# The opening of a hybrid attention and RG-LRU block in an order written by hand: x first, modulation on ScalarE, bias as a weight column, fewer activation tables

## The chip, the core and the metric

One core of a Trainium2 chip runs the whole program. The metric is the device time of one execution in microseconds (us); less is better. TensorE is called PE, VectorE DVE, ScalarE ACT, GpSimd POOL, SyncE SP, as the profile does. Of each kernel several executions are timed, and one execution is profiled, which leaves a trace.

## What is computed

The block takes x (1024 tokens by 1024 channels), a condition vector c and a set of weights. The part that the change touches is the beginning: the RMS norm, the modulation by c, and the first columns of the big projection.

```python
mod = c @ w_ada + b_ada
shift, scale, gate = jnp.split(mod, 3, axis=-1)
h = rmsnorm(x, norm_g) * (1.0 + scale[:, None, :]) + shift[:, None, :]
proj = h @ w_in                       # 1024 x 6656
q, k, v, g_attn, xr, g_rnn, m_attn, m_rnn = jnp.split(proj, SPLIT_POINTS, axis=-1)
q = partial_rope(q, positions)        # angles of positions: sin and cos of 8 frequencies
k = partial_rope(k, positions)
...                                   # window attention with sinks, conv and RG-LRU, gates
x = x + gate[:, None, :] * (merged @ w_out)
return rmsnorm(x, final_g)
```

All values are f32.

## The kernel before, in words

**Products.** A product in full precision is made of three products of the type fp32r. Each operand is split into a high part (a cast) and a low part (the operand less its high part): `wh` and `wl` of the weights (`cast`, L101 and L103 on ACT; `rest`, L107 and L109 on DVE), `hh` and `hl` of the activations. A chunk of 128 output columns over 128 input channels is wh·hh, wl·hh and wh·hl, each for two halves of 512 tokens: six matmuls (`mm_k`, L168). In names of tiles an a or a b behind hh or hl is the half of tokens, and a number at the end counts tiles.

**The opening, L178 to L355.** SP loads four small arrays (positions, frequencies, a table of parameters `pk`, the row c), then the eight tiles of x (128 tokens by 1024 channels each), weights of the modulation `w_ss` and weights of the projection. Every x tile is squared and summed (L309 on ACT for even tiles, L311 on DVE for odd ones), the mean is taken (L314), its root on ACT (L316), the reciprocal and the scaling on DVE (L317, L318). PE transposes the tiles 128 by 128 (L323), ACT copies the results to `xT[kc]` (L325): channels kc·128 to kc·128+127 on the partitions, tokens along the row. DVE computes the rope angles in 29 small instructions (L239 to L299), ACT their sine (L328), and DMAs on POOL's queue write the table out (L331 on).

Then, for each of the eight channel chunks kc, `modulate` (L217) makes shift and scale: two DVE instructions, each multiplying a tile of `w_ss` by c and summing along the row (L220), and two single-column ones that add the bias and the norm gain (L225, L228). DVE applies them to `xT[kc]` (L344), ACT casts the two halves to hh (L347), DVE subtracts for hl (L349), and PE adds this chunk's share to three chunks of output columns, the *starts*: `w_main` 0 and 1 (the keys) and 2 (the first of the queries, scaled by 0.125). For kc up to 5 that is twelve matmuls with hh and six with hl at a time; kc 6 and 7 come last, one start after the other. A chunk kc takes 18 matmuls.

The order in which each engine of the opening runs its instructions is decided by a scheduler, which works from a model of durations and may also pull later instructions forward. From L360 on (`manual_schedule`) every engine runs in the order in which the code is written.

**What follows.** POOL makes differences of `xT` (`differences`, L381 to L384). The weights of v are split; `now` (L578 on) applies the rope to the starts (ACT L424, L425; DVE L426, L430, L431); `v_product` multiplies for v (L1259 to L1261: 96 matmuls in two calls); then the bulk of the projection is done with products of half-size blocks (`product`, L505), in fixed slots, and attention, RG-LRU and the output follow.

A few lines of the opening's end in before:

```python
for hf in range(2):
    last = A.copy(hh[kc][hf], xT[kc][:, SL[hf]])
for hf in range(2):
    V.tensor_tensor(out=hl[kc][hf], in0=xT[kc][:, SL[hf]], in1=f32(hh[kc][hf]), op=ALU.subtract)
if kc < 6:
    for w, ps in starts:
        mm_k(ps, w, kc, terms="h")
    for w, ps in starts:
        mm_k(ps, w, kc, terms="l")
```

Of the kernel before, what the change touches and what calls it, by code (L numbers as in the profile page):

```python
# [12 lines left out]
F32 = mybir.dt.float32  # L13
# [3 lines left out]
BF16 = mybir.dt.bfloat16  # L17
# [5 lines left out]
P = 128  # L23
S = 1024
# [27 lines left out]
def tile_hybrid_block(ctx, tc, x, pk, rows, posr, posi, invf, c_row, w_ss, w_gate, w_main, w_v,  # L52
# [4 lines left out]
    def dma(dst, src, eng=nc.sync):  # L57
        dst, src = (a.bitcast(F32) if a.dtype == F32R else a for a in (dst, src))
        return eng.dma_start(dst, src)  # L59
# [26 lines left out]
    def pcol(base, i):  # L86
        return pk_t[:, base + i:base + i + 1]
# [85 lines left out]
    def new_ps():  # L173
        t = psm.tile([P, 1024], F32, tag="main", name="pmain")
        return [t[:, SL[0]], t[:, SL[1]]]


    with ExitStack() as st:  # L178
        sp = st.enter_context(tc.tile_pool(name="start", bufs=1, side="right"))
        posr_t = sp.tile([P, 64], I32, name="posr_t")  # L180
        dma(posr_t[:], posr)
        invf_t = sp.tile([P, 1], F32, name="invf_t")
        dma(invf_t[:], invf)
        dma(pk_t[:], pk)
        make_identity(nc, ident)

        c_row_t = sp.tile([1, D], F32, tag="xt", name="c_row_t", bufs=10)
        dma(c_row_t[:], c_row)
        one_row = sp.tile([1, P], F32, name="one_row")
        V.memset(one_row[:], 1.0)  # L190
        c_bc = sp.tile([P, D], F32, name="c_bc")
        for hf in range(2):
            T.matmul(bk[hf], one_row[:], c_row_t[:, SL[hf]], start=True, stop=True)
            A.copy(c_bc[:, SL[hf]], bk[hf])

        xt = []
        starts = []
        wada = {}

        def load_ss(kc):  # L200
            for a in range(2):
                wa_t = sp.tile([P, D], F32, tag="xt", name="wada", bufs=10)
                dma(wa_t[:], w_ss[a * D + kc * P:a * D + (kc + 1) * P, :])
                wada[kc, a] = wa_t

        def load_xt(i):
            t = sp.tile([P, D], F32, tag="xt", name="xt", bufs=10)
            dma(t[:], x[i * P:(i + 1) * P, :])
            xt.append(t)

        mods = sp.tile([P, 16], F32, name="mods")
        gsc = sp.tile([P, 8], F32, name="gsc")
        bsc1 = sp.tile([P, 8], F32, name="bsc1")
        V.tensor_scalar(out=bsc1[:], in0=pk_t[:, PK_BSC:PK_BSC + 8], scalar1=1.0, scalar2=None,
                        op0=ALU.add)

        def modulate(kc):  # L217
            for a in range(2):
                jk = sp.tile([P, D], BF16, tag="junk2", name="jk")
                V.scalar_tensor_tensor(out=jk[:], in0=wada[kc, a][:], scalar=1.0, in1=c_bc[:],  # L220
                                       op0=ALU.mult, op1=ALU.mult,
                                       accum_out=mods[:, a * 8 + kc:a * 8 + kc + 1])
            shf = mods[:, kc:kc + 1]
            g1 = gsc[:, kc:kc + 1]
            V.scalar_tensor_tensor(out=g1, in0=mods[:, 8 + kc:9 + kc],  # L225
                                   scalar=bsc1[:, kc:kc + 1], in1=pcol(PK_NG, kc),
                                   op0=ALU.add, op1=ALU.mult)
            V.tensor_tensor(out=shf, in0=shf, in1=pcol(PK_BSH, kc), op=ALU.add)  # L228
            return g1, shf

        def load_start(i):
            w = load_w(w_main[i], 0.125 if i == 2 else 1.0)
            starts.append((w, new_ps() if i < 2 else bk[2:]))

        def tiny(name, n=64):
            return sp.tile([P, n], F32, name=name)
# [14 lines left out]
        def sub(name, a, b, n=64):  # L251
            t = tiny(name, n)
            V.tensor_tensor(out=t[:], in0=a, in1=b, op=ALU.subtract)
            return t
# [10 lines left out]
        def weighted(name, which):  # L265
            t = tiny(name)
            for i, (piece, unit) in enumerate(pieces):
# [4 lines left out]
                else:  # L272
# [1 line left out]
                                           op0=ALU.mult, op1=ALU.add)  # L274
            return t

        sa = weighted("sa", 0)
        ra = rnd("ra", sa[:], 1.0)
        fa = sub("fa", sa[:], ra[:])
        sb = weighted("sb", 1)  # L280
        tt = tiny("tt")
        V.tensor_tensor(out=tt[:], in0=fa[:], in1=sb[:], op=ALU.add)
        rt = rnd("rt", tt[:], 1.0)
        ft = sub("ft", tt[:], rt[:])
        sc_ = weighted("sc_", 2)
        V.scalar_tensor_tensor(out=sc_[:], in0=a00[:], scalar=1.0 / (2.0 * math.pi),
                               in1=sc_[:], op0=ALU.mult, op1=ALU.add)
        trn = sp.tile([P, 2, 64], F32, name="trn")
        V.tensor_tensor(out=trn[:, 1, :], in0=ft[:], in1=sc_[:], op=ALU.add)
        V.tensor_scalar(out=trn[:, 0, :], in0=trn[:, 1, :], scalar1=0.25, scalar2=None,  # L290
                        op0=ALU.add)
        trf = trn[:].rearrange("p a t -> p (a t)")
        r2 = rnd("r2", trf, 1.0, 128)
        V.tensor_tensor(out=trf, in0=trf, in1=r2[:], op=ALU.subtract)
        V.tensor_scalar(out=trf, in0=trf, scalar1=2.0 * math.pi, scalar2=3.1415925,
                        op0=ALU.mult, op1=ALU.min)
        V.tensor_scalar(out=trf, in0=trf, scalar1=-3.1415925, scalar2=None, op0=ALU.max)
        for i in range(8):
            load_xt(i)  # L299
        load_ss(0)  # L300
        load_start(0)
        ss = tiny("ss", 8)
        rr = tiny("rr", 8)
        for hf in range(2):
            for i in range(hf * 4, hf * 4 + 4):
                junk = sp.tile([P, D], BF16, tag="junk", name="junk")
                r1 = rr[:, i:i + 1]
                if i % 2 == 0:
                    A.activation(junk[:], xt[i][:], AF.Square, accum_out=ss[:, i:i + 1])  # L309
                else:  # L310
                    V.scalar_tensor_tensor(out=junk[:], in0=xt[i][:], scalar=1.0,  # L311
                                           in1=xt[i][:], op0=ALU.mult, op1=ALU.mult,
                                           accum_out=ss[:, i:i + 1])
                V.tensor_scalar(out=r1, in0=ss[:, i:i + 1], scalar1=1.0 / D, scalar2=EPS,  # L314
                                op0=ALU.mult, op1=ALU.add)
                A.activation(r1, r1, AF.Sqrt)  # L316
                V.reciprocal(r1, r1)  # L317
                xsc = V.tensor_scalar(out=xt[i][:], in0=xt[i][:], scalar1=r1, scalar2=None,  # L318
                                      op0=ALU.mult)
            for kc in range(KC):  # L320
                pt = bk[kc % (2 if hf else 4)]
                for j in range(4):
                    T.transpose(pt[:, j * P:(j + 1) * P],  # L323
                                xt[hf * 4 + j][:, kc * P:(kc + 1) * P], ident[:])
                A.copy(xT[kc][:, SL[hf]], pt)  # L325
        csn = sp.tile([P, 3, 64], F32, name="csn")
        with tc.issue_after(xsc.ins):
            A.activation(csn[:, 0:2, :].rearrange("p a t -> p (a t)"), trf, AF.Sin)  # L328
        V.tensor_scalar(out=csn[:, 2, :], in0=csn[:, 1, :], scalar1=-1.0, scalar2=None,
                        op0=ALU.mult)  # L330
        for a in range(3):  # L331
            dma(cs_d[a * 8:(a + 1) * 8, :].rearrange("f (b t) -> (f b) t", b=16),
                csn[:, a, :], G)
        dma(cs4_d, cs_d.unsqueeze(1).to_broadcast([24, 4, S]), G)

        for kc in range(KC):
            if kc == 0:
                load_start(1)
                load_start(2)
            else:  # L340
                load_ss(kc)
            with tc.issue_after(xsc.ins):
                g1, shf = modulate(kc)
            V.tensor_scalar(out=xT[kc][:], in0=xT[kc][:], scalar1=g1, scalar2=shf,  # L344
                            op0=ALU.mult, op1=ALU.add)
            for hf in range(2):
                last = A.copy(hh[kc][hf], xT[kc][:, SL[hf]])  # L347
            for hf in range(2):
                V.tensor_tensor(out=hl[kc][hf], in0=xT[kc][:, SL[hf]], in1=f32(hh[kc][hf]),  # L349
                                op=ALU.subtract)  # L350
            if kc < 6:
# [4 lines left out]
        done = None  # L356
        for w, ps in starts:
            with tc.issue_after(done.ins) if done else nullcontext():
                for kc in (6, 7):
                    done = mm_k(ps, w, kc)  # L360


    order = ExitStack()
    ET = mybir.EngineType
    order.enter_context(tc.manual_schedule(engines={ET.PE, ET.Activation, ET.DVE, ET.Pool,
                                                    ET.SP}))


    hn = pool(h_ctx, "hn")
# [905 lines left out]
    for i in range(4):  # L1275
        differences(i)
    place(pairs)
    rv = [load_half(w_v[i // 2][:, SL[i % 2]]) for i in range(4)]
# [309 lines left out]
def arrange(inputs):  # L1588
# [46 lines left out]
```

## Time and profile before

| what | value |
|---|---|
| median of 3 executions | 944.1 us (943.53 to 944.49) |
| the profiled execution | 944.47 us |
| its span, first to last instruction | 942.5 us, so 1.97 us lie outside |
| granted TensorE clock | 0.999 |
| PE busy over the span | 908.1 us, 96% |

The page of the profile gives the busy time of each engine, then its busy tenths in 40 slices of 23.6 us, then the groups of instructions by line. A row of a group has the line, the engine, the operation, out<-in by the program's names, partitions x elements, a count, the busy us, the mean ns of one, and after the second bar the idle time of the engine just before them with what ended it. A row of the timeline has the start in us, the duration in us, engine, line, operation, the names, and in brackets the idle time before it and its releaser. A row of the windows has the stretch, its length, then busy us and (count) for PE, PEld, DVE, ACT and POOL, the granted clock, the busy share of the DMA engines and GB/s.

### The profile page before, as it was taken

To read this page: it belongs to the slowest core of one execution; us is meant where nothing else is said; L and a number is where in the kernel's file an instruction comes from. 1 tells how busy PE (TensorE), PEld (TensorE's weight loads), DVE (VectorE), ACT (ScalarE), POOL (GpSimd) and SP (SyncE) were. 2 spreads that over 40 slices of the span, in tenths; PEclk is the share of its full clock that TensorE was granted. 3 is DMA by queue.
4 is the path that set the end of the run, shared out by engine and by line. 5 is a ranking of instruction groups with operands and counts; after the bars stand their busy time and mean duration, and the time that the engine had idled before them with its cause. 6 is when DMAs were issued, how large, how long until landed. Compare 5 with 4: busy or idle time off the path is not lost.

```text
span 942.5 us, 12419 instructions
## 1 busy us (share of the span) xinstructions
PE 908.1 (96%) x4261; PEld 750.6 (80%) x4261; DVE 688.8 (73%) x1068; ACT 528.8 (56%) x1036; POOL 89.7 (10%) x129
## 2 busy tenths in 40 slices
PE   5899999999999999999999999989999999999997
PEld 3689777788888788888888778867888888887886
DVE  7977798876668955984688677888999737656522
ACT  7434654455556755866585775877888632212311
POOL 1056000000000000000000000233333300000000
PEclk9999999999999999999999999999999999999999
DMA  8923565753332433352334237897666286436321
GB/s 312 370 68 152 184 223 202 268 189 125 112 112 96 139 136 100 133 212 80 122 112 168 100 134 261 278 342 251 215 198 187 67 304 219 168 118 235 128 79 67
DMA packets 84275, 164.19 MB, mean 174 GB/s; under 512 B 12771, under 2 KB 33251, under 8 KB 84214
## 3 DMA queue, kind: packets, MB, share of 16 engines
q1 hardware_dynamic: 83350, 161.09, 49.8%
q0 software_dynamic: 720, 2.07, 0.6%
q8 instruction: 33, 0.54, 0.2%
q14 instruction: 28, 0.23, 0.1%
q10 hardware_dynamic: 144, 0.26, 0.1%
HBM read 114.00 MB, written 49.78 MB: 174 GB/s over the span
## 4 chain that ended last, share of the span: by engine, by line
PE 75%; ACT 4%; DMA 4%; DVE 4%; issue 2%; SPq 0%; POOL 0%; DVEq 0%; ACTq 0%
PE bk L505 39%; PE rp L168 12%; PE rp L1500 5%; PE pgate L778 5%; PE pmain L1500 4%; PE pmain L168 4%; PE s_ps L1016 3%; PE pv L1088 3%; PE pt L1054 1%; DMA dv<-dv_d 1%; DMA ks<-k_d 1%; DMA r<-w_rp 1%; ACT wh L101 1%; DMA r<-w_main 1%; DVE nl L390 1%
## 5 line engine op out<-in xcount | busy, mean ns | idle before, releaser
L505 PE MATMUL bk<-nh,wl 128*128 128x512 f32 x368 | 143.7, 391 | 2.0 <-DVE wl L107 1.9
L505 PE MATMUL bk<-nh,wh 128*128 128x512 f32 x368 | 143.4, 390 | 0.0
L505 PE MATMUL bk<-nl,wh 128*128 128x512 f32 x368 | 143.2, 389 | 0.0
L107 DVE TENSOR_TENSOR wl<-r,wh 128x512 fp32r<-128x512 f32 x108 | 79.1, 736 | 16.5 <-ACT wh L101 16.5
L101 ACT CAST wh<-r 128x512 fp32r<-128x512 f32 x108 | 66.5, 618 | 33.5 <-DMA r<-w_ap 11.3
L505 PEld LDWEIGHTS bk<-nh,wl 128*128 128x128 f32 x368 | 69.1, 188 | 17.7 <-DVE wl L107 3.1
L505 PEld LDWEIGHTS bk<-nh,wh 128*128 128x128 f32 x368 | 69.1, 188 | 15.2 <-ACT wh L103 0.9
L505 PEld LDWEIGHTS bk<-nl,wh 128*128 128x128 f32 x368 | 69.1, 188 | 14.3
L505 PE MATMUL bk<-hh,wl 128*128 128x512 f32 x184 | 71.7, 390 | 0.4 <-DVE wl L107 0.4
L505 PE MATMUL bk<-hl,wh 128*128 128x512 f32 x184 | 71.6, 389 | 0.0
L505 PE MATMUL bk<-hh,wh 128*128 128x512 f32 x184 | 71.6, 389 | 0.0
L107 DVE TENSOR_TENSOR wl<-ws,wh 128x512 fp32r<-128x512 f32 x80 | 54.1, 683 | 4.0 <-ACT wh L101 4.0
L101 ACT CAST wh<-ws 128x512 fp32r<-128x512 f32 x80 | 48.2, 616 | 4.8 <-DVE ws L527 3.0
L1040 ACT ACTIVATE p<-p,small 128x129 f32<-128x129 f32 x128 | 50.1, 400 | 0.0
L59 POOL DMA_DIRECT2D yh_d<-yh x1 | 0.6, 583 | 482.3 <-ACT yh L835 482.3
L505 PE MATMUL bk<-hha,wl 128*128 128x512 f32 x92 | 36.4, 395 | 5.9 <-DVE wl L107 4.4
L505 PEld LDWEIGHTS bk<-hh,wl 128*128 128x128 f32 x184 | 34.5, 188 | 7.9 <-DVE wl L107 0.8
L505 PEld LDWEIGHTS bk<-hh,wh 128*128 128x128 f32 x184 | 34.5, 188 | 7.2
L505 PEld LDWEIGHTS bk<-hl,wh 128*128 128x128 f32 x184 | 34.5, 188 | 7.1
L1016 PE MATMUL s_ps<-ks,qs 128*128 128x256 f32 (+1 forms) x256 | 37.5, 289 | 0.0
L1517 ACT ACTIVATE o<-xo 128x1024 f32<-128x1024 f32 (+2 forms) x10 | 8.9, 889 | 48.4 <-DVE xo L1516 48.4
L505 PE MATMUL bk<-hla,wh 128*128 128x512 f32 x92 | 35.9, 390 | 0.0
(338 smaller groups left out, 2231.7 us busy)
## 6 DMA issues: line engine op xcount, KB each, us to landing
r<-w_main SPq DMA_DIRECT2D x100, 256.0 KB, 4.0
wada<-w_ss SPq DMA_DIRECT2D x16, 512.0 KB, 8.6
qs<-q_d SPq DMA_DIRECT2D x16, 512.0 KB, 5.4
ks<-k_d SPq DMA_DIRECT2D x24, 192.0 KB, 4.1
xt<-x SPq DMA_DIRECT2D x8, 512.0 KB, 7.2
q_d<-rhi SPq DMA_DIRECT2D x16, 256.0 KB, 3.5
q_d<-rlo SPq DMA_DIRECT2D x16, 256.0 KB, 3.3
wg<-w_gate SPq DMA_DIRECT2D x8, 512.0 KB, 5.0
```

What stands on the lines that cost most here:

```text
L101: A.copy(dst[0][:], src)
L107: V.tensor_tensor(out=dst[1][:], in0=src, in1=f32(dst[0][:]), op=ALU.subtract)
L168: mm = T.matmul(ps[hf], ww, xx[kc][hf], start=(kc == 0 and ww is w_h and xx is xh), stop=(kc == KC - 1 and xx is xl))
L390: V.tensor_tensor(out=nl[t][:], in0=xT[t][:], in1=f32(nh[t][:]), op=ALU.subtract)
L505: W["pe"] = T.matmul(ps, ww[:, c], b[kc][xx_], start=(first and kc == 0 and i == 0), stop=(kc == 3 and i == 2), skip_group_check=not first)
L778: W["pe"] = T.matmul(ps[:, SL[hf]], ww[:, c0:c0 + P], xx_[:, SL[hf]], start=(ic == 0 and i == 0), stop=(ic == 1 and i == 2))
L1016: W["pe"] = T.matmul(o, qs[:, j, qc], ks[:, b, k0 + (0 if n else P):k0 + 256], start=(b == 0), stop=(b == 1))
L1040: A.activation(px[:, j, :], px[:, j, :], AF.Exp, bias=sm[:, 0, j:j + 1], accum_out=sm[:, 1, j:j + 1])
L1054: W["pe"] = T.transpose(pt[:, j, :], px[:, j, 0:P], ident[:])
L1088: W["pe"] = T.matmul(pv[:], b, m[:].rearrange("p j q -> p (j q)"), start=(i == 0), stop=(i == len(prods) - 1))
L1500: T.matmul(ps[:, sl], lhs[k][th][:, ts_], w[:, sl], start=(k == 0 and w is h_ and lhs is mh), stop=(k == KC - 1 and lhs is ml))
L1517: A.activation(o[:, sl], xo[:, sl], AF.Square, accum_out=fs[:, i:i + 1])
```

## The change

The whole opening is put under `manual_schedule`, so that every engine runs it in the order written. In that order:

- The four small loads go to ACT's DMA queue; on SP the eight x tiles are first, then `w_ss` for kc 0, the first halves of the starts' weights, `w_ss` for kc 1 and 2; the rest is issued in the loop.
- The row of `w_ss` has 1025 numbers, the last one the bias, and c has a 1 behind it, so the row sum contains the bias: the addition L228 and the preparation L214 go. The tiles xt and wada are 1025 wide (rows of 4100 bytes).
- The squares of tiles 1 and 7 move from DVE to ACT, which does six of eight. A root of one number (L224 of the changed kernel) stands ahead of them.
- Shift and scale are applied on ACT: `cast_h` makes hh for both halves directly from the raw `xT` with Identity, scale and bias, and then a third, 1024 wide Identity writes `xT` itself, from which DVE's `low_h` subtracts. DVE's L344 goes.
- Of the 29 small rope instructions 21 move into `turns()`, at the end of kc = 3 on DVE; the sine and the table's DMAs move into `table()` at kc = 4.
- The second token half's transposes of chunks 2 to 7 move into the loop, four after each chunk's matmuls; `modulate` runs two chunks ahead; the second halves of the starts' weights are split in kc = 1, 2, 3.
- Being under the same manual order, the matmuls of v stay behind the starts.

```diff
+    order.enter_context(tc.manual_schedule(engines={ET.PE, ET.Activation, ET.DVE, ET.Pool,
+                                                    ET.SP}))
...
+        dma(c_row_t[:], c_row, A)
+        dma(posr_t[:], posr, A)
+        dma(invf_t[:], invf, A)
+        dma(pk_t[:], pk, A)
...
+                wa_t = sp.tile([P, D + 1], F32, tag="xt", name="wada", bufs=10)
...
+        for i in range(8):
+            load_xt(i)
+        load_ss(0)
+        load_wh(0, 0)
+        load_wh(1, 0)
+        load_ss(1)
+        load_wh(2, 0)
+        load_ss(2)
...
+        A.activation(root[:], one_row[:, 0:1], AF.Sqrt)
+        c_bc = sp.tile([P, D + 1], F32, name="c_bc")
+        V.memset(c_bc[:, D:], 1.0)
...
-            V.tensor_tensor(out=shf, in0=shf, in1=pcol(PK_BSH, kc), op=ALU.add)
...
-            V.tensor_scalar(out=xT[kc][:], in0=xT[kc][:], scalar1=g1, scalar2=shf,
-                            op0=ALU.mult, op1=ALU.add)
...
+        def cast_h(kc):
+            for hf in range(2):
+                A.activation(hh[kc][hf], xT[kc][:, SL[hf]], AF.Identity,
+                             scale=gsc[:, kc:kc + 1], bias=mods[:, kc:kc + 1])
+            A.activation(xT[kc][:], xT[kc][:], AF.Identity, scale=gsc[:, kc:kc + 1],
+                         bias=mods[:, kc:kc + 1])
...
+        for a in range(2):
+            modulate(0, a)
+        high(0, 0)
+        cast_h(0)
+        for i in range(3):
+            if i:
+                high(i, 0)
+            low(i, 0)
...
+        for a in range(2):
+            modulate(1, a)
+        for kc in range(KC):
+            low_h(kc)
+            if kc == 0:
+                load_ss(3)
+                for i in range(3):
+                    load_wh(i, 1)
+            if kc < 4:
+                load_ss(kc + 4)
+            elif kc == 4:
+                rv = [load_half(w_v[i // 2][:, SL[i % 2]]) for i in range(3)]
+            if kc in (1, 2, 3):
+                high(kc - 1, 1)
+            if kc + 1 < KC:
+                cast_h(kc + 1)
+            if kc + 2 < KC:
+                for a in range(2):
+                    modulate(kc + 2, a)
+            if kc in (1, 2, 3):
+                low(kc - 1, 1)
+                starts[kc - 1][0].append(W0[kc - 1, 1])
+            if kc == 3:
+                turns()
+            if kc == 4:
+                table()
             if kc < 6:
                 for w, ps in starts:
                     mm_k(ps, w, kc, terms="h")
                 for w, ps in starts:
                     mm_k(ps, w, kc, terms="l")
+            if kc + 2 < KC:
+                turn(1, kc + 2)
+                evict(1, kc + 2)
...
-    a["w_ss"] = np.ascontiguousarray(w_ada[:, :2048].T)
+    a["w_ss"] = np.concatenate([w_ada[:, :2048].T, b_ada[:2048, None]], axis=1)
```

The order of DVE where the loop begins (jk is the unused product of a modulation sum, mods and gsc are shift and scale), in before:

```order
L220 SCALAR_TENSOR_TENSOR jk,mods<-wada,c_bc 128x1024
L107 TENSOR_TENSOR wl<-r,wh 128x512
L220 SCALAR_TENSOR_TENSOR jk,mods<-wada,c_bc 128x1024
L228 TENSOR_TENSOR mods<-mods,pk_t 128x1
L107 TENSOR_TENSOR wl<-r,wh 128x512 x2
L225 SCALAR_TENSOR_TENSOR gsc<-mods,bsc_219,pk_t 128x1
L107 TENSOR_TENSOR wl<-r,wh 128x512
L109 SCALAR_TENSOR_TENSOR wl<-r,wh 128x512
L344 TENSOR_SCALAR xT<-xT,gsc,mods 128x1024
L220 SCALAR_TENSOR_TENSOR jk,mods<-wada,c_bc 128x1024
L349 TENSOR_TENSOR hla_160<-xT,hha_158 128x512
```

The same place on DVE in the changed kernel:

```order
L235 SCALAR_TENSOR_TENSOR jk,mods<-wada,c_bc 128x1025 x2
L239 SCALAR_TENSOR_TENSOR gsc<-mods,pk_t 128x1
L107 TENSOR_TENSOR wl<-r,wh 128x512 x2
L109 SCALAR_TENSOR_TENSOR wl<-r,wh 128x512
L235 SCALAR_TENSOR_TENSOR jk,mods<-wada,c_bc 128x1025 x2
L239 SCALAR_TENSOR_TENSOR gsc<-mods,pk_t 128x1
L367 TENSOR_TENSOR hla_160<-xT,hha_158 128x512
```

Five low halves of weights and the affine L344 stood ahead of the first hl; now three low halves and the whole modulation of the next chunk do.

The same engine later, at the end of kc = 3 in the changed kernel, where hl_175 is the low part of chunk 4 (the 21 small instructions, of which the first three and the last two are shown in two pieces):

```order
L235 SCALAR_TENSOR_TENSOR jk,mods<-wada,c_bc 128x1025 x2
L239 SCALAR_TENSOR_TENSOR gsc<-mods,pk_t 128x1
L109 SCALAR_TENSOR_TENSOR wl<-r,wh 128x512
L278 TENSOR_SCALAR sa<-t_260 128x64
L281 SCALAR_TENSOR_TENSOR sa<-t_264,sa 128x64
L281 SCALAR_TENSOR_TENSOR sa<-t_268,sa 128x64
```

```order
L305 TENSOR_TENSOR trn<-trn,r_575 128x128
L306 TENSOR_SCALAR trn<-trn 128x128
L308 TENSOR_SCALAR trn<-trn 128x128
L367 TENSOR_TENSOR hl_175<-xT,hh_174 128x512 x2
L235 SCALAR_TENSOR_TENSOR jk,mods<-wada,c_bc 128x1025 x2
```

Before, nothing but a modulation, the affine and now and then a low half of a weight stood between the hl of two chunks.

On ACT, at the beginning of the loop in the changed kernel:

```order
L101 CAST wh<-r 128x512
L360 ACTIVATE hha_158<-xT,mods,gsc 128x512
L360 ACTIVATE hhb_159<-xT,mods,gsc 128x512
L362 ACTIVATE xT<-xT,mods,gsc 128x1024
L101 CAST wh<-r 128x512
L103 ACTIVATE wh<-r 128x512
L360 ACTIVATE hha_162<-xT,mods,gsc 128x512
```

The high parts of the second and third start's weights stand behind the three modulating instructions of chunk 0.

More of the change, by code (lines that the diff above doesn't have):

```diff
@@ L180, in tile_hybrid_block @@
         posr_t = sp.tile([P, 64], I32, name="posr_t")
-        dma(posr_t[:], posr)
         invf_t = sp.tile([P, 1], F32, name="invf_t")
[L183 to L194, printed above, removed]
+        c_row_t = sp.tile([1, D], F32, name="c_row_t")
+        dma(c_row_t[:], c_row, A)
+        dma(posr_t[:], posr, A)
+        dma(invf_t[:], invf, A)
+        dma(pk_t[:], pk, A)
         xt = []
         starts = []
-        wada = {}
+        wada, halfw = {}, {}
         def load_ss(kc):
             for a in range(2):
-                wa_t = sp.tile([P, D], F32, tag="xt", name="wada", bufs=10)
+                wa_t = sp.tile([P, D + 1], F32, tag="xt", name="wada", bufs=10)
                 dma(wa_t[:], w_ss[a * D + kc * P:a * D + (kc + 1) * P, :])
@@ L211, in tile_hybrid_block @@
         mods = sp.tile([P, 16], F32, name="mods")
         gsc = sp.tile([P, 8], F32, name="gsc")
[L213 to L229, printed above, removed]
@@ L326, in tile_hybrid_block @@
[L326 to L334, printed above, removed]
@@ L355, in tile_hybrid_block @@
                     mm_k(ps, w, kc, terms="l")
-        done = None
+            if kc + 2 < KC:
+                turn(1, kc + 2)
+                evict(1, kc + 2)
         for w, ps in starts:
[L358 to L366, printed above, removed]
+            for kc in (6, 7):
+                mm_k(ps, w, kc)
     hn = pool(h_ctx, "hn")
```

179 lines of the change are left out of this document (120 added, 59 removed).

## The prediction

> **What bounds the kernel now.** I read the page first: the engines' totals and PE's tenths over the span.
>
> ```profile
> PE 908.1 (96%) x4261; PEld 750.6 (80%) x4261; DVE 688.8 (73%) x1068; ACT 528.8 (56%) x1036; POOL 89.7 (10%) x129
> PE   5899999999999999999999999989999999999997
> ```
>
> PE is busy nearly everywhere but in the first slices, which are the opening. So the end moves by the change in PE's idle time, and the opening is where that can change. The windows split it at the first matmul of a start, the last one, the first L505 product and a point behind it.
>
> ```profile
> 0.00:28.21 28.21, 16.38 (x69) 11.44 (x69) 23.49 (x77) 22.00 (x44) 3.35 (x10) 1.00 0.88 326
> 28.21:67.97 39.76, 37.30 (x170) 29.74 (x169) 35.33 (x70) 12.23 (x22) 9.40 (x12) 1.00 0.57 213
> 67.97:99.32 31.35, 31.35 (x219) 29.38 (x218) 25.30 (x27) 17.68 (x28) 18.60 (x13) 1.00 0.35 127
> 99.32:119.82 20.50, 17.30 (x74) 13.36 (x72) 14.76 (x23) 12.15 (x21) 0.00 (x0) 1.00 0.63 217
> 119.82:942.50 822.68, 805.78 (x3735) 666.70 (x3735) 589.92 (x875) 464.74 (x924) 58.39 (x95) 1.00 0.50 168
> ```
>
> After 119.82 PE is busy for 805.78 of 822.68 us, in an order that the change leaves alone, so I let a shift at 119.82 stand to the end. In the loop (28.21 to 67.97) PE idles only 2.46 us, with DVE almost as full (35.33 of 39.76).
>
> The groups of DVE and ACT up to 68 us price what is moved.
>
> ```profile
> L220 DVE SCALAR_TENSOR_TENSOR jk<-wada,c_bc 128x1024 bf16<-128x1024 f32 x16 | 19.5, 1218 | 0.0
> L344 DVE TENSOR_SCALAR xT<-xT,gsc,mods 128x1024 f32<-128x1024 f32 x8 | 6.5, 806 | 0.0
> L349 DVE TENSOR_TENSOR hl<-xT,hh 128x512 fp32r<-128x512 f32 x8 | 5.3, 685 | 0.7 <-ACT hh L347 0.7
> L109 DVE SCALAR_TENSOR_TENSOR wl<-r,wh 128x512 fp32r<-128x512 f32 x2 | 1.4, 685 | 0.0
> L228 DVE TENSOR_TENSOR mods<-mods,pk_t 128x1 f32<-128x1 f32 x8 | 1.2, 153 | 0.0
> ```
>
> ```profile
> L101 ACT CAST wh<-r 128x512 fp32r<-128x512 f32 x8 | 4.8, 624 | 3.7 <-PE pmain L168 3.7
> L309 ACT ACTIVATE junk<-xt 128x1024 bf16<-128x1024 f32 x4 | 4.2, 1048 | 4.4 <-DMA xt<-x 4.4
> L316 ACT ACT_TABLE_LOAD x2 | 2.6, 1283 | 0.0
> L347 ACT CAST hha<-xT 128x512 fp32r<-128x512 f32 x4 | 2.5, 622 | 8.7 <-DVE xT L344 8.7
> ```
>
> And the timeline fixes the paces.
>
> ```profile
> 0.81 0.39 SPq L59 DMA_DIRECT2D posr_t<-posr  x1
> 2.58 4.41 SPq L59 DMA_DIRECT2D xt<-x  x8
> 4.98 0.22 DVE L273 SCALAR_TENSOR_TENSOR sb<-t,sb 128x64 f32<-128x64 f32 x1
> 5.12 0.22 DVE L273 SCALAR_TENSOR_TENSOR sc__255<-t,sc__255 128x64 f32<-128x64 f32 x1
> 6.28 0.22 DVE L253 TENSOR_TENSOR fa<-sa,ra 128x64 f32<-128x64 f32 x1
> 7.02 0.23 DVE L253 TENSOR_TENSOR ft<-tt,rt 128x64 f32<-128x64 f32 x1
> 20.34 0.75 DVE L318 TENSOR_SCALAR xt<-xt,rr 128x1024 f32<-128x1024 f32 x1
> 25.31 0.69 DVE L107 TENSOR_TENSOR wl<-r,wh 128x512 fp32r<-128x512 f32 x1
> 25.91 0.69 DVE L109 SCALAR_TENSOR_TENSOR wl<-r,wh 128x512 fp32r<-128x512 f32 x1
> 27.21 1.15 PE L323 MATMUL bk<-ident,xt 128*128 128x128 f32 x8 [0.19 <-ACT xT L325]
> 27.53 0.62 ACT L347 CAST hha<-xT 128x512 fp32r<-128x512 f32 x1
> 28.05 0.62 ACT L347 CAST hhb<-xT 128x512 fp32r<-128x512 f32 x1
> 28.21 0.74 PE L168 MATMUL pmain<-hha,wh 128*128 128x512 f32 x2
> 32.07 0.81 DVE L344 TENSOR_SCALAR xT<-xT,gsc,mods 128x1024 f32<-128x1024 f32 x1
> 36.49 0.81 DVE L344 TENSOR_SCALAR xT<-xT,gsc,mods 128x1024 f32<-128x1024 f32 x1
> 65.31 0.61 PE L168 MATMUL bk<-hh,wh 128*128 128x512 f32 x2
> 67.58 0.62 PE L168 MATMUL bk<-hl,wh 128*128 128x512 f32 x2
> ```
>
> From 65.31 to 67.58 PE starts ten matmuls, 0.227 us each. From 27.21 to 28.21 it does eight transposes: 0.12 each. A chunk of the loop takes 4.42 us from L344 to L344 (32.07 to 36.49), and its 18 matmuls only 18·0.227 = 4.1: the loop before goes at DVE's pace. Small DVE instructions that need the one before start 0.25 apart (three steps from 6.28 to 7.02), independent ones 0.14 (4.98 to 5.12). Two low halves start 0.6 apart (25.31 to 25.91), two casts on ACT 0.52 (27.53 to 28.05).
>
> **The change part by part.** I walked the changed kernel's queues in their written order with these durations.
>
> First, the start of the matmuls, now 28.21. The x loads are issued at 0.81 in place of 2.58: 1.77 earlier. On ACT two squares are added (2·1.05) and the later table loads (1.28 each) go or move behind. But the norm of the last tiles is now a chain of ACT and DVE in strict order (root, reciprocal, scaling, and next square behind an eviction), and in the walk the last scaling starts at 22.2, not 20.34. Behind it, before, DVE did five low halves at 0.6 (3.0) and L344 (0.72 to the next) until the cast; these 3.7 to 3.8 us go. The start is 28.21 + 1.9 − 3.8, about 26.2: **−2.0**. If the last scaling stays at 20.34 it is −3.8; if the lead of x is worth nothing, −0.2. I take the walk, since each step in it has a row. The two sums of 1025, one column longer, I price at the same 1218 ns; L228 (0.15, hidden or not) is small.
>
> Second, the loop. Its matmuls are 8·18·0.227 = 32.7. The transposes of six chunks are now in it: 24·0.12 = 2.9. The rest is stalls, by place:
>
> - Chunk 0. The second start waits for its weights: `wh` is cast behind the three modulating instructions (2·0.52 in pace, and the wide one at the square's 1.05), then DVE's low half: 0.3 + 0.9 + 0.3 = 1.5. Then the hl of chunk 0 stands on DVE behind two low halves (2·0.6) and the whole modulation of chunk 1 (2·1.25 + 0.15), while PE has 12·0.227 = 2.7 of hh work: PE waits 2.5, and 0.4 between the two halves. In before the first hl followed one sum (L220), so no such wait. Together 4.4.
> - Chunks 1 to 3. DVE needs 2·0.61 + 2·1.25 + 0.15 + 0.6 = 4.4 to 4.5, PE 4.1 + 0.49: even, 0.
> - Chunk 4. Its hl stands behind the modulation of chunk 5, a low half and the 21 instructions of `turns`. These depend on each other nearly throughout: 4.7 us by the walk, at 0.25 for most. PE waits 0.3 + 3.0 + 0.4 = 3.7. What is late next are the sine and the modulation of chunk 6, which PE reaches 4.6 later, so no more is lost.
> - Chunks 6 and 7. The last hl waits for ACT's wide Identity: 0.4 + 1.1 + 0.4 = 1.9.
>
> Together about 9.9, where before had 2.46, and with 24 v matmuls in its stalls. So the starts end at 26.2 + 32.7 + 2.9 + 9.9 = 71.7, against 67.9 (the last pair at 67.58): **+3.8**. No row shows an Identity with scale and bias from the partitions; a Copy without them is 0.62 for 512. Between 0.62 and the 1.05 of 1024 columns I take 0.62; 0.3 more each would give +1.5 at the end, and 0.06 less nothing. DVE's waits taken as 0.7 us kinder or harsher at each of the two big stalls move it by 1.4 either way.
>
> Third, behind the starts.
>
> ```profile
> 51.12 0.28 PE L1260 MATMUL bk<-wl,hha 128*128 128x256 f32 x1
> ...
> 53.76 0.28 PE L1261 MATMUL bk<-wh,hla 128*128 128x256 f32 x1
> ```
>
> ```profile
> 68.28 0.63 ACT L103 ACTIVATE wh<-r 128x512 fp32r<-128x512 f32 x1 [2.14 <-PE bk L168]
> 73.51 1.67 DVE L431 TENSOR_TENSOR c<-c 64x512 f32<-64x512 f32 x1
> 87.85 0.68 DVE L431 TENSOR_TENSOR c<-c 64x512 f32<-64x512 f32 x1
> ```
>
> ```profile
> L505 PE MATMUL bk<-hha,wl 128*128 128x512 f32 x6 | 2.6, 428 | 3.1 <-DVE wl L107 1.6 <-DVE wl L109 1.5
> ```
>
> Before, 24 matmuls of v ran inside the loop (the rows from 51.12 to 53.76 are 23 of them at 0.12, the order puts one ahead). Now they come behind the starts: PE has 24·0.12 = 2.9 more there, so its own sum is 3.8 + 2.9 = 6.7 late at 99.32. But there PE waits 3.1 us for low weights that DVE makes, and those hang on ACT and DVE, which are released by the starts' end (2.14 at 68.28) and are 3.8 late, not 6.7. PE alone would be 6.7 − 3.1 = 3.6 late, the other chain 3.8. On top I put 0.4 because POOL's `differences` begin later and run beside more of the rope's DVE work (the same L431 takes 1.67 at 73.51 and 0.68 at 87.85, when POOL is idle). The later of the two chains counts: **+4.2**.
>
> [...]
>
> The sum for the profiled execution: 944.47 + 4.2 = 948.7. Its time outside the span (1.97) stays. The median of the runs shown is 0.37 below it, so I predict **948.3**.
>
> **The rivals.**
>
> *DVE relief wins; faster.* The loop before goes at DVE's 4.42 per chunk, and the change takes L344 (0.72) and L228 (0.07 in pace) from each. If the waits that I count in the order do not appear, because DVE is ahead of PE by then, the starts end at 26.2 + 32.7 + 2.9 = 61.8 plus what remains of stalls. The point from which it decides: stalls in the loop below 9.9 − 4.2 = 5.7 us. With 2.5 (before's own) the end is 944.1 − 3.2 = 941. For it: 4.42 against 4.1, and ACT idle for 8.7 behind L344. Against: `turns` and the modulation ahead of the first hl are in a fixed order that nothing overtakes.
>
> *Half the size.* If the 21 instructions run at the pace of independent ones (0.14), the stall in chunk 4 is 2.3 smaller: about 946, within 0.2% (about 1.9 us, what a measurement of this kernel can tell from no change).
>
> *The rows of 4100 bytes are slow.*
>
> ```profile
> wada<-w_ss SPq DMA_DIRECT2D x16, 512.0 KB, 8.6
> ```
>
> Six `w_ss` loads are 3.1 MB of what the opening's 28.21 us carry at 326 GB/s with the DMA engines busy for 0.88. At half their speed 3.1 MB more cost 9.6 us; about half is covered by the norm and by two chunks of lead: +4.5 more, about 953. No row has such a width. [...]
>
> *The opening doesn't get earlier.* If x lands no sooner, because c's and pk's loads or the transfer itself limit it, the first matmul is at 28: about 950.
>
> **How the numbers follow.** My forecast, 947 to 951 with the Identity and the two stalls at their ends: 0.68. Half the size, 945 to 946.5: 0.12. DVE relief, 939 to 942: 0.09. Slow rows, 952 to 955: 0.07. Opening not earlier, 949 to 951: 0.04. The range leaves out DVE relief and slow rows and a little at both edges: 945.0 to 952.0. Faster by over 0.2% is DVE relief, 0.09; within 0.2% (942.2 to 946.0) most of half the size and a tail, 0.13; slower 0.78.
>
> **What would show it.** In the changed kernel's trace: x loads on SP at 0.8; the first start matmul at 26.2; PE waiting 2.5 before the first hl (<-DVE hl L367) and 3.0 before that of chunk 4, behind a row of L278 to L308 on DVE; an end of the starts near 71.7; the first L505 behind 103; two table loads, not four. A wait of PE on ACT (hh) instead of DVE, or an end of the starts before 66, proves me wrong. If PE waits on DVE and DVE on a DMA of wada, it is the third rival.

## The result, and the profile after

The changed kernel takes **954.39 us** (954.01 to 955.14), the kernel before 944.3 beside it: a ratio of **1.0109** with a 95% interval of 1.0092 to 1.0127. That is 10.1 us slower, where 4.2 were forecast and the range ended at 952.0. The profiled execution took 954.01, its span 952.3, so 1.7 lie outside; span against span the loss is 9.8.

The windows of the changed kernel, cut at the same events as before: first start matmul, end of the starts (its last pair, issued at 77.39, and 2·0.227), first product of half-size blocks, a point behind it. The columns are those of the table before.

```profile
0.00:29.55 29.55, 12.53 (x44) 8.26 (x44) 15.16 (x44) 16.44 (x37) 0.70 (x6) 0.94 0.68 248
29.55:77.84 48.29, 43.24 (x168) 31.82 (x169) 40.94 (x82) 30.62 (x40) 11.80 (x16) 0.89 0.59 208
77.84:112.01 34.17, 34.17 (x243) 32.23 (x241) 28.77 (x31) 20.01 (x31) 18.94 (x13) 1.00 0.38 140
112.01:132.50 20.49, 18.76 (x83) 15.22 (x82) 14.45 (x23) 11.45 (x21) 0.00 (x0) 1.00 0.62 206
132.50:952.30 819.80, 803.74 (x3728) 664.85 (x3726) 587.67 (x872) 463.12 (x921) 58.42 (x95) 1.00 0.50 168
```

The first window is 1.34 longer, not 2.0 shorter; the loop 48.29 against 39.8 (before's ends at 68.03 by the same count). So the starts end 9.8 later, and that is the whole loss. The stage behind them has 2.8 more of PE work (34.17), the v matmuls, and the first product comes 12.7 late. PE then waits once for low weights instead of twice, and the wait that ended at 119.82 before ends at 130.45 (the row below), 10.6 later; at the end 9.8 are left. Two clocks in this table are below 1.00, and none was in the table before.

```profile
130.45 0.50 PE L595 MATMUL bk<-hha,wl 128*128 128x512 f32 x1 [1.73 <-DVE wl L107]
```

Where the first window went, on DVE and ACT and in the list of DMA issues (KB, median us to landing). The first row is before's, the others are the changed kernel's:

```profile
3.44 0.25 DVE L241 TENSOR_SCALAR ang<-posf,invf_t 128x64 f32<-128x64 f32 x1 [0.74 <-DMA invf_t<-invf]
```

```profile
5.62 0.19 ACT L329 ACTIVATION_READ_ACCUMULATOR junk<-xt 128x1 f32 x1
6.21 0.20 DVE L247 CAST posf<-posr_t 128x64 f32<-128x64 int32 x1 [5.14 <-DMA posr_t<-posr]
9.30 0.26 DVE L249 TENSOR_SCALAR ang<-posf,invf_t 128x64 f32<-128x64 f32 x1 [2.90 <-DMA invf_t<-invf]
10.94 0.15 DVE L333 TENSOR_SCALAR rr<-ss 128x1 f32<-128x1 f32 x1
```

```profile
posr_t<-posr ACTq DMA_DIRECT2D x1, 32.0 KB, 4.8
invf_t<-invf ACTq DMA_DIRECT2D x1, 0.5 KB, 7.4
```

The frequencies, half a kilobyte, take 7.4 us to land on ACT's queue while SP's queue carries x. DVE waits for them until 9.30 (3.44 in before), then does the rest of the eight small rope instructions, and only at 10.94 takes the first mean of the norm, whose square ACT had ready at 5.8.

Where the loop went, on PE and ACT, and the clock:

```profile
29.55 0.80 PE L168 MATMUL pmain<-hha,wh 128*128 128x512 f32 x1 [2.20 <-ACT hha L360]
...
36.59 0.49 PE L168 MATMUL pmain<-hla,wh 128*128 128x512 f32 x1 [0.77 <-DVE hla L367]
...
58.66 1.58 PE L168 MATMUL pmain<-hl,wh 128*128 128x512 f32 x4 [2.30 <-DVE hl L367]
...
71.44 1.10 PE L168 MATMUL pmain<-hl,wh 128*128 128x512 f32 x2 [1.02 <-DVE hl L367]
```

```profile
L362 ACT ACTIVATE xT<-xT,mods,gsc 128x1024 f32<-128x1024 f32 x8 | 10.0, 1244 | 0.3
L360 ACT ACTIVATE hh<-xT,mods,gsc 128x512 fp32r<-128x512 f32 x8 | 6.1, 806 | 0.0
```

```profile
22.00:29.50 7.50, 3.57 (x21) 2.73 (x19) 5.76 (x13) 6.23 (x15) 0.00 (x0) 0.78 0.61 195
29.50:36.50 7.00, 6.13 (x12) 3.56 (x12) 4.41 (x9) 3.52 (x5) 0.00 (x0) 0.50 1.01 401
36.50:58.00 21.50, 19.37 (x88) 15.04 (x88) 20.59 (x53) 16.82 (x23) 0.00 (x0) 1.00 0.76 266
58.00:64.00 6.00, 5.23 (x17) 4.00 (x18) 5.93 (x12) 3.73 (x6) 1.82 (x3) 0.72 0.05 16
```

The waits stand where they were forecast: chunk 0, chunk 4 behind `turns`, chunk 7. New are the Identity's 0.81 and 1.24, and the clock. It is granted at 0.50 through chunk 0's matmuls with hh, which start 0.43 apart instead of 0.227, and at 0.72 behind the stall of chunk 4. So PE waits 0.77 for chunk 0's hl and not the 2.5 of the forecast, since its matmuls ahead of it take twice as long; for chunk 4's hl it waits 2.30, where 3.0 were forecast.

### The profile page after: what moved, and what is told of

Read it like the earlier page. It is cut to its first block, busy times and chain, and to the rows that moved or that the text cites. A ratio compares the mean times of both kernels' runs of the same rounds, so it can differ in the third digit from the quotient of the medians.

```text
span 952.3 us, 12406 instructions
## 1 busy us (share of the span) xinstructions
PE 912.4 (96%) x4261; PEld 752.4 (79%) x4261; DVE 687.0 (72%) x1048; ACT 541.6 (57%) x1047; POOL 89.9 (9%) x129
## 4 chain that ended last, share of the span: by engine, by line
PE 70%; DVE 10%; DMA 9%; ACT 6%; issue 3%; SPq 0%; POOL 0%; DVEq 0%; ACTq 0%
PE bk L595 37%; PE rp L168 8%; PE rp L1590 5%; PE pgate L868 5%; PE pmain L1590 4%; PE pmain L168 3%; PE s_ps L1106 2%; PE pv L1178 2%; DVE jk L235 1%; DMA tt<-tr_d 1%; DMA wo<-w_out 1%; PE pt L1144 1%; DMA dv<-dv_d 1%; DMA smr<-smr_d 1%; DVE wl L107 1%
## 5 line engine op out<-in xcount | busy, mean ns | idle before, releaser
L107 DVE TENSOR_TENSOR wl<-r,wh 128x512 fp32r<-128x512 f32 x108 | 82.8, 772 | 16.2 <-ACT wh L101 16.1
L698 ACT ACTIVATE c<-bk 128x512 f32<-128x512 f32 x31 | 18.5, 596 | 30.5 <-PE bk L595 30.5
```

The lines of the kernel that those rows point to most:

```text
L107: V.tensor_tensor(out=dst[1][:], in0=src, in1=f32(dst[0][:]), op=ALU.subtract)
L698: A.activation(t["t"], s(), AF.Tanh, scale=0.5)
```

## The experiments

Each is the changed kernel with one edit, unless its heading says otherwise. Of each the first start matmul and the end of the starts are read from its one profiled execution, the time from several; before stood at 943.57 beside the first four, at 944.17 beside the next four, at 943.87 beside the last. Each ratio is the one on record, up to 0.0013 off the quotient of the two medians. Single executions of one kernel of this family lie up to 5 us apart (951.33 to 956.64 in the second below), so a difference of 1 in a median decides nothing. Nor is the profiled execution always a middle one: it was the slowest of four in the first experiment and the fastest in the second and third. From the end of the starts to the end of the span the profiles take 872.1 to 876.8 us (874.5 in before and in the changed kernel), so the end of the starts shows the opening's gain or loss more sharply than the time does.

**The four small loads first.**

```diff
-        dma(c_row_t[:], c_row, A)
-        dma(posr_t[:], posr, A)
-        dma(invf_t[:], invf, A)
-        dma(pk_t[:], pk, A)
+        dma(posr_t[:], posr)
+        dma(invf_t[:], invf)
+        dma(pk_t[:], pk)
+        dma(c_row_t[:], c_row)
```

> The four small loads go back to SP, ahead of x. Theory 'late frequencies': in the changed kernel DVE waits 2.90 us for invf, landed at 9.3, because its packets queue among those of x, and everything of the norm stands behind it on DVE. Then with the small loads first DVE's first mean moves from 10.94 to about 7.7, the first start matmul from 29.55 to about 26.5, and the end by about 3: 951.4. Rival 'x paces the norm': x is issued 1.8 later than in the changed kernel, the norm goes at the pace of x, the first matmul stays at 29 or later: 954 to 956. Rival 'cold clock': PE's granted clock of 0.5 from 26 to 36.5 is what costs; it would stay, and the end with it: 954.

Measured 954.15, 1.0107 (1.0085 to 1.0129). The frequencies are there at once (3.46 in place of 9.30):

```profile
3.46 0.25 DVE L249 TENSOR_SCALAR ang<-posf,invf_t 128x64 f32<-128x64 f32 x1 [0.66 <-DMA invf_t<-invf]
```

The first start matmul moves only to 27.95, since x is 1.8 later, and the starts end at 77.49. In this execution the low clock came back (0.62 from 36.5 to 40), over the end of chunk 0 and in chunk 1, and took most of the gain back. None of the theories had the outcome: the wait was there, its removal alone did not show in the end.

**The rope's first eight instructions to chunk 3.**

```diff
             if kc == 3:
+                angles()
                 turns()
```

> The loads stay on ACT's queue; the eight small rope instructions that need posr and invf leave the head of DVE's queue and go in front of the other 21 at the end of chunk 3. Theory 'late frequencies': the first mean comes at about 6.1, the first start matmul near 26, 3.3 earlier; the wait in chunk 4 grows by 8 x 0.25 = 2.0: end about 1.3 earlier, 953. Rival 'x paces the norm': the first matmul stays near 29 and the end is 2 later: 956.4.

Measured 954.72, 1.0121 (1.0103 to 1.014); first start matmul at 26.17, end of the starts 77.54.

```profile
26.17 0.80 PE L168 MATMUL pmain<-hha,wh 128*128 128x512 f32 x1 [2.24 <-ACT hha L362]
...
57.14 2.25 PE L168 MATMUL pmain<-hl,wh 128*128 128x512 f32 x4 [4.24 <-DVE hl L369]
```

With the frequencies out of DVE's way the opening takes the 26.2 that I had forecast for the change, and the stall of chunk 4 grows from 2.30 to 4.24, by the 8·0.25. Both effects are as the first theory has them; the end is not, at 954.7 and not 953 (the profiled execution, 951.33, was the fastest of the four).

**PE kept busy with transposes that nobody reads.**

```diff
+        warm(ps0[0], 12)
         for kc in range(2):
             turn(1, kc)
             evict(1, kc)
+        warm(ps0[0], 12)
...
+                if kc == 4:
+                    warm(bk[0], 14)
```

> Adds 38 transposes of the identity that nobody reads (12 before the second half's transposes, 12 ahead of the first start matmul, 14 between the hh and hl matmuls of chunk 4), all in stretches where PE waits. Theory 'cold clock, partly hidden': the clock stays at 1.0 from 26 on; in chunk 0 the 2.4 us that the twelve hh matmuls save are waited for DVE's hl instead (hl at 36.5), at most 0.7 is left of them; in chunks 4 and 5 the slow stretch from 58.7 to 64 cost 2.3 and is saved: end 2 to 3 earlier, 952. Rival 'cold clock is all': both stretches save in full, 5 earlier: 949. Rival 'the clock doesn't follow PE's busy time': no change, or later by the transposes that overrun, 954 to 956.

Measured 955.14, 1.0113 (1.0094 to 1.0131). In its profile the clock is 1.00 from 26 to 29.5 and behind the stall of chunk 4, yet 0.74 to 0.77 from 29.5 to 36.5. The starts end at 75.07, but 1.2 of that is that the frequencies landed 1.2 earlier in this execution. Inconclusive: the clock answered in part, the time did not.

**The bias as separate additions.** `w_ss` back to 1024 columns, L228 back.

> w_ss back to 1024 columns, tiles of 4096 bytes a row; the bias is added by a small instruction per chunk (0.15, 0.07 in pace), as before. Theory 'rows of 4100 bytes cost nothing here' (no wait of DVE for wada over 0.3 in the changed kernel): 954.4, within 1, with the small additions 0 to 0.5 later. Rival 'slow rows': the loads queue ahead of the starts' weights and of x, 3 or more earlier: below 951.5.

Measured 956.05, 1.013 (1.0113 to 1.0148), the end of the starts 79.49. Wider rows cost the kernel nothing: without them it is no faster, rather 1.7 slower, and DVE waits for no tile of `w_ss` in either. A tile does land a little later with them (6.0 us in the changed kernel, 4.5 here, medians of 16 tiles), but 8.6 in before, with narrow rows. This rival falls.

**Without `turns`.** The 21 instructions are left out and the angles set to a constant, so this kernel does not compute the rope.

```diff
+        V.memset(trn[:], 0.5)
...
-            if kc == 3:
-                turns()
```

> The 21 rope instructions at the end of chunk 3 are left out (the angles are a constant, so the rope is not computed rightly); all else as in the changed kernel. It prices the stall in chunk 4 and what follows from it. Theory 'the stall cools the clock': in the changed kernel PE waits 2.3 there and the matmuls from 58.7 to 64 then run at a lower clock for 1.6 more; both go, and the last start matmul ends 3.5 to 4.5 earlier than 77.8, at about 73.8: 950.5. Rival 'the wait alone': 2.3 to 2.5 earlier, 952. Rival 'DVE's total is the limit': the stall comes back in chunks 5 to 7, less than 1 earlier.

Measured 952.59, 1.0077 (1.0061 to 1.0093), the end of the starts 74.99, which is 2.85 earlier. PE's clock from 52 to 64, first of the changed kernel and then of this one:

```profile
52.00:64.00 12.00, 9.30 (x35) 6.62 (x34) 11.27 (x36) 9.64 (x14) 1.82 (x3) 0.86 0.40 150
```

```profile
52.00:64.00 12.00, 11.71 (x57) 9.01 (x55) 8.27 (x17) 11.15 (x14) 1.81 (x3) 1.00 0.42 154
```

Here the wait and the slow stretch behind it both go: 57 matmuls in place of 35. Against the pace of 0.227, chunks 4 and 5 lose 1.0 us instead of 5.4. Chunk 0 loses 1.0 more in this execution, where the slow clock comes back over its matmuls with hl (0.57 from 36 to 40), and PE waits again for the hl of chunks 6 and 7. So the stall and its echo are worth 4.4 by themselves, as the first theory has it, and the 2.85 at the end of the starts are what is left of them.

**Shift and scale back on DVE.**

```diff
-            for hf in range(2):
-                A.activation(hh[kc][hf], xT[kc][:, SL[hf]], AF.Identity,
-                             scale=gsc[:, kc:kc + 1], bias=mods[:, kc:kc + 1])
-            A.activation(xT[kc][:], xT[kc][:], AF.Identity, ...)
+            V.tensor_scalar(out=xT[kc][:], in0=xT[kc][:], scalar1=gsc[:, kc:kc + 1],
+                            scalar2=mods[:, kc:kc + 1], op0=ALU.mult, op1=ALU.add)
+            for hf in range(2):
+                A.copy(hh[kc][hf], xT[kc][:, SL[hf]])
```

> Shift and scale go back to DVE (one instruction of 1024 per chunk, 0.72 in pace) and ACT makes two plain casts; everything else as in the changed kernel. Theory 'the move to ACT helps, only less than it could': DVE gets 8 x 0.72 = 5.8 more in a loop that it paces nearly throughout, the waits for hl grow by 2 to 3 in all and the end is 2 to 3 later: 957. Rival 'the move is what hurts' (Identity with scale and bias takes 0.81 and 1.24 where the cast takes 0.62): the end is earlier than 953.

Measured 957.58, 1.0129 (1.0112 to 1.0145), the end of the starts 79.24. The wait for the hl of chunk 4 is twice as long, since DVE has more ahead of it:

```profile
60.55 0.79 PE L168 MATMUL pmain<-hl,wh 128*128 128x512 f32 x1 [4.48 <-DVE hl L366]
```

The move to ACT helps by about 3 in the medians (1.9 by the ratios, 1.4 at the end of the starts), even at the Identity's price. So the move is not what hurts.

**All of the rope in the opening's gaps.** The two small loads first on SP, `some(n)` emits the next n rope instructions:

```diff
+        some(12)
         square(0)
         square(1)
         mean(0)
+        some(1)
         norm(0)
...
         mean(1)
+        some(4)
...
-            if kc == 3:
-                turns()
```

> All 29 rope instructions go back to the opening: the two small loads that they need are first on SP, the first 12 instructions run before x is there and the other 17 one to six at a time where DVE waits for ACT's roots; c and the parameters stay on ACT's queue. Theory 'two DVE placements and their echo on the clock are the loss': first start matmul at 27.2, no wait in chunk 4, last start matmul ends near 73 (71 without any slow clock), end 949.5. Rival 'rope in the norm delays it as much': first start matmul at 29.5 or later, end 952 or later.

Measured **948.76**, 1.005 (1.0035 to 1.0066); first start matmul 27.16, the starts end at 71.17. The first theory holds to within 0.8 us in the time and comes out 1.8 earlier at the end of the starts, although the clock is low in chunk 0 here too. PE's waits up to the end of chunk 5, but for one of 0.20:

```profile
27.16 0.80 PE L168 MATMUL pmain<-hha,wh 128*128 128x512 f32 x1 [2.69 <-ACT hha L380]
34.20 0.49 PE L168 MATMUL pmain<-hla,wh 128*128 128x512 f32 x1 [1.17 <-DVE hla L396]
```

Leaving out `turns` alone gave 1.8 in the medians, moving the two loads alone 0.8 (below); together, with the rope's 29 instructions in DVE's gaps, they give 5.6, and 6.7 at the end of the starts.

**The loop's order mended as well.** On top of the last: eight squares on ACT, mean, root and reciprocal for two tiles at a time, and in the loop

```diff
                 for w, ps in starts:
                     mm_k(ps, w, kc, terms="h")
+                turn(1, kc + 2)
+                evict(1, kc + 2)
                 for w, ps in starts:
                     mm_k(ps, w, kc, terms="l")
-            if kc + 2 < KC:
-                turn(1, kc + 2)
-                evict(1, kc + 2)
         for w, ps in starts:
             for kc in (6, 7):
-                mm_k(ps, w, kc)
+                mm_k(ps, w, kc, terms="h")
+            for kc in (6, 7):
+                mm_k(ps, w, kc, terms="l")
```

> The same, with these moves of order: all eight squares on ACT, mean, root and reciprocal for two tiles at a time; weights' high parts ahead of the wide Identity of chunk 0; half of the modulation of chunk 1 behind the hl of chunk 0; the second half's transposes between a chunk's hh and hl matmuls; hl of chunks 6 and 7 behind both hh; 12 unread transposes ahead of the first start matmul. From the durations seen, the first start matmul comes at 23.6 and the last one ends near 66 if the clock holds: end 942.5, 1.5 earlier than before. Rival 'slow clock anyway': two stretches of 3 at half pace, end 944 to 946. Rival 'x paces the opening': first start matmul at 26 or later, end 945 to 948.

Measured 943.43, 0.9992 (0.9977 to 1.0007): level with before, and 0.9 above the expected time. First start matmul 23.38, the starts end at 66.00, as expected to 0.3.

**The two small loads alone.** Only posr and invf to SP, ahead of x.

> The changed kernel with posr and invf alone moved to SP, ahead of x (which starts 0.9 later); c and the parameters stay on ACT's queue. It prices the wait of DVE for the frequencies by itself, without the rope's other move. Theory 'late frequencies': first start matmul at 27.2 in place of 29.55, last start matmul ends at 74 to 76 (77.8 in the changed kernel), end 951 to 952.5. Rival 'no effect beyond the opening' (as the medians of the first two of my kernels, 954.2 and 954.7, would have it): PE's slow clock in the first chunks eats it, the end at 954 or later.

Measured 953.6, 1.0101 (1.0086 to 1.0116); first start matmul 27.08 as expected, the starts end at 75.31, 2.5 earlier. The median gained only 0.8, so the rival keeps a part: what an earlier start brings is not all kept to the end in every execution.

**The best order, without and with the filler.** On top of the reordered kernel: the last rope instructions into DVE's wait for weights, all three high parts of weights ahead of the wide Identity of chunk 0.

> As the next one, without the 12 unread transposes ahead of the first start matmul. Theory 'the clock follows PE's idle time and shows where PE itself is late': PE idles 2.2 more before the first start matmul at 23.6, the first chunk's matmuls run at half pace, 0.2 more for each of the 18 less what is waited for anyway: last start matmul ends 1 to 3 later than with the filler, end 942.5 to 944.5. Rival 'the filler does nothing': within 0.5 of it.

> As the reordered kernel, with the rope's last instructions on DVE moved into its wait for the second start's weights, and all three weights' high parts ahead of the wide Identity of chunk 0. From the durations seen, the hl of chunk 0 comes 0.9 earlier and the hh of chunk 1 too; last start matmul ends at 64.3 (66.0 there, 68.0 in before): end 941.7, 2.5 below before. Rival 'the loop is at its floor': last start matmul at 66, end 943.4 again.

Without the filler **941.02**, 0.9971 (0.9959 to 0.9983); with it 941.55, 0.9977 (0.9966 to 0.9988). Both beat the kernel before. The filler does nothing that shows: without it the clock is 1.00 all through the starts too. The windows of the one without:

```profile
0.00:23.81 23.81, 11.72 (x45) 7.83 (x45) 14.53 (x51) 17.11 (x35) 0.70 (x6) 1.00 0.76 285
23.81:64.60 40.79, 38.29 (x168) 29.08 (x169) 37.38 (x64) 31.09 (x42) 11.73 (x16) 1.00 0.72 260
64.60:98.77 34.17, 34.17 (x243) 32.23 (x241) 28.75 (x31) 20.02 (x31) 18.95 (x13) 1.00 0.38 139
```

The loop now takes 40.79, with PE busy 38.29: 2.5 us of idle, as in before, though the transposes are in it; and it begins 4.4 earlier.

**Chunk 0's order alone.** Weights' high parts ahead of the wide Identity, half of the modulation of chunk 1 behind the hl of chunk 0.

> The changed kernel with chunk 0's order alone mended: all high parts of weights ahead of the wide Identity, and only half of the modulation of chunk 1 ahead of the hl of chunk 0. It prices the order that put 4.4 into my sum for chunk 0. Theory 'order': hl comes 2.3 earlier, the wait for it goes and the last start matmul ends 1 to 1.5 earlier than 77.8 : 953. Rival 'the slow clock hides it': the hh matmuls run at half pace until 35 anyway, no gain, 954.4.

Measured 952.26, 1.0093 (1.0076 to 1.0111), the starts end at 75.43. Of these 2.4, 1.1 is an earlier first matmul (28.44; the frequencies landed 1.1 earlier); the other 1.3 came with the order. The wait for chunk 0's hl is gone, as the first theory had it, and chunk 0 loses 2.4 in place of 4.8; part of that is the clock, low until 32.9 here and until 36.45 in the changed kernel. Chunk 1 gives 0.8 of it back and chunks 4 and 5 together 0.4, the stall of chunk 4 being 2.99 here.

## Why the prediction was wrong

The direction and the places of the stalls were right; the size was short by 5.6 us in the span. Rounding apart the sums come out as written (the parts give 26.3 for the start and 10.0 for the stalls, and before's starts end at 68.03, not 67.9). By its steps:

- **The start of the matmuls: this step failed.** I credited the move of x with 1.77 and priced the move of the four small loads to ACT's queue at nothing, without naming what waits behind them. On DVE eight rope instructions stand ahead of the norm, and they need the frequencies, which it read at 9.30 instead of 3.44. So −2.0 became +1.34, an error of 3.3. With those eight instructions out of the way (second experiment) the first matmul comes at 26.17, the forecast 26.2: the rest of that working held, the last scaling included (21.9 for 22.2). My fourth rival, an opening that is not earlier, got 0.04 and had another cause: c's and pk's loads or the transfer holding back x. But x was early, ACT's first square starting at 4.66 in place of 6.53; it was DVE that was held.
- **The loop's stalls: right places, undersized.** I had 9.9; what the loop takes beyond 0.227 a matmul and 0.12 a transpose is 12.7. With PE's rows cut at the transposes behind chunks 0, 3, 4 and 5 (38.45, 52.17, 60.70, 66.75) it is 4.8 for chunk 0 (4.4 forecast), 0.0 for chunks 1 to 3 (0), 4.0 for chunk 4 (3.7), 1.5 for chunk 5 (0) and 2.4 for chunks 6 and 7 (1.9). The Identity, which I put at 0.62 for 512 columns, takes 0.81, and 1.24 for the wide one; what makes it slower than the cast is not shown.
- **The clock: not in the prediction at all.** From 60.35 to 63.76, at 0.50, some 1.7 us went (half of 3.41, an estimate), most of the loss of chunk 5 among them. In chunk 0 the half pace hid mostly behind DVE's hl: of its own instructions ahead of that hl DVE waited only for ACT (2.76 for a high part of weights), not for PE.
- **Behind the starts: right in size, not in its terms.** 2.9 of v work more, as forecast. But of the 3.1 of waits only 1.3 went (one wait of 1.73 is left). The shift of 9.8 at the end of the starts is 10.6 at 130.45 and 9.8 again at the end; what made and took back the 0.8 is not shown, and the 0.4 for POOL cannot be told apart in it.
- **The rivals.** Independent pace in `turns` (0.14) did not happen: the 21 instructions took 4.97 us, from 52.95 to 57.92, and their stall was 2.30 with a slow stretch behind it. Slow rows of 4100 bytes fell with the fourth experiment. DVE relief is real (2 to 3 us by the sixth), but only an order without these waits shows it: the two best kernels are that rival with further moves, at 941 to 941.6, as it had it.

What stays open is how much the clock costs by itself. Removing the late frequencies moved the first matmul earlier by 1.6, 2.5 and 3.4 in three kernels, and the median by 0.2 and 0.8 earlier and 0.3 later; in the profiles of the first and the last of these a low clock that came back and the longer stall of chunk 4 took it back, while in the second the starts do end 2.5 earlier. That is shown for those executions. That it explains the medians is argued. Why the frequencies land so late beside x, their place on ACT's queue, their rows of 4 bytes or the traffic, was not taken apart either.

## What to carry to other kernels

When a load changes its queue, look up who reads it first and what stands behind that reader on its engine: beside x on the other queue the smallest of these loads took longer to land than a larger one (7.4 us for 0.5 KB, 4.8 for 32 KB). In an order written by hand each engine is a list without overtaking (the hl of chunk 4 stood behind the 4.97 us of `turns`), so a chain of small dependent instructions belongs where its engine waits anyway, and another chunk's preparation behind, not ahead of, what the bottleneck needs next. A stall of the matrix engine can cost more than its length: behind the 2.30 of chunk 4 the granted clock was 0.50 for 3.41 us.

## What the runs showed of the hardware

A DMA of 0.5 KB in 128 rows took 7.4 us to land on ACT's queue, and one of 32 KB 4.8, beside x on SP's; ahead of x the frequencies were read at 3.46. The landing also varied: DVE got the frequencies at 8.1 to 9.3 in the six kernels that load and read them so.

The clock is on record only from 22.8 us on in before and in the changed kernel; ahead of that a window's 1.00, in the prediction's table too, stands for no record. In both the transposes start 0.21 apart up to there and 0.11 behind it, so at about half the pace. From there on the changed kernel's trace has two stretches at 0.50 ahead of the one in which the span ends: 10.24 and 3.41 us, the first three times as long as the second. Before's has none ahead of its end (1.00 from 22.75 to 940). In the changed kernel (a stretch ahead of the fall, then the two low ones):

```profile
22.80:26.21 3.41, 1.63 (x13) 1.19 (x12) 2.07 (x6) 2.33 (x7) 0.00 (x0) 1.00 0.47 152
26.21:36.45 10.24, 7.28 (x17) 4.30 (x17) 7.34 (x15) 6.57 (x11) 0.00 (x0) 0.50 0.98 364
60.35:63.76 3.41, 3.41 (x12) 2.73 (x11) 3.34 (x9) 1.96 (x3) 1.34 (x3) 0.50 0.08 29
```

No single wait of PE between 22 and 29.55 was as long as the shorter of these stretches (the longest was 2.20), and PE's busy time in the 3.41 us ahead of a fall does not decide it alone. The clock fell behind 1.81 of 3.41 in the first experiment's kernel (its matmuls from 31.03 to 32.31 start 0.43 apart), and stayed at 1.00 behind 1.81 in before and 1.79 in the best kernel, in this order:

```profile
22.12:25.53 3.41, 1.81 (x13) 1.13 (x11) 2.99 (x7) 2.33 (x7) 0.00 (x0) 1.00 0.62 201
```

```profile
22.75:26.16 3.41, 1.81 (x14) 1.27 (x14) 3.41 (x9) 3.41 (x8) 0.00 (x0) 1.00 0.96 347
```

```profile
20.06:23.47 3.41, 1.79 (x16) 1.55 (x14) 2.90 (x6) 2.76 (x6) 0.00 (x0) 1.00 0.49 154
```

What separates these is not shown.
